# Decoder step on one core: affine maps of the decay gate and PSUM copies of the attention put on ScalarE instead of VectorE

## The chip, the cores and the metric

The kernel runs on one core of one Trainium2 chip. A core has a matrix engine (TensorE, PE in the profile, with its weight loads as PEld), VectorE (DVE), ScalarE (ACT), GpSimd (POOL) and SyncE (SP), which here issues all DMAs. The engines run their own queues in order and meet at semaphores. Matrix products are written to banks of PSUM; everything else lives in SBUF or in DRAM. The metric is the device time of one execution in microseconds, as the median of several runs.

## What is computed

One layer of a decoder for 512 prompt tokens and 8 x 8 new tokens (64 more columns), model width 1024, all in float32. Cut to what the change touches:

```python
u = x * (1 + sc1) + sh1
proj = u @ w_in            # qa, ka, va, qh, fh, ih, ogh, gate_a, gate_b
# attention: three groups (window, dilation) of four heads each
for gi, (win, dil) in enumerate(ATTN_GROUPS):
    # prompt: banded causal attention per residue; also returns the log-sum-exp
    # new tokens: keys of the cache and of the new tokens
    o_g, lse_g = attention(q_g, k_g, v_g)
attn = sum over groups of softmax(lses) * outs
# gated linear recurrence, eight heads
hq = silu(qh)
f = lb + (1.0 - lb) * sigmoid(fh)
hk = 1.0 - f
S_t = diag(f_t) S_{t-1} + hk_t v_t^T;  o_t = S_t^T hq_t
# merge by sigmoid gates, layer norm, squared-ReLU MLP, layer norm
```

Besides the layer's result, the keys and values of the prompt's last tokens and the caches moved on by the new tokens are outputs, so keys are needed with tokens along the partitions ("token-major") as well as the other way.

## The kernel before

Activations are kept with channels along the 128 partitions and the 576 tokens (`NT`) along the free axis, in two halves of 288 (`HF`). A float32 product is made of three products in a faster format: an operand is split into a rounded part and its rest (`whi`, `wlo` for weights, `uh`, `ul` for activations). `whi` is a copy on ACT, `wlo` a subtraction on DVE; both must be done before PE can begin a block of weights. `split` does this, and `ahead` calls it up to two blocks before the block runs.

The first part of the program runs over `flat`, a list of blocks of 128 columns of `w_in`, then of the two branch matrices. `run_block` does one: two halves of 24 matmuls into a PSUM bank tagged `lin` (two banks), each followed by `evac`, which takes the result out of PSUM, and after both an `after` that hands over side work. Of the attention, each group has `q_block`, `v_tokens` and `k_block`; of the recurrence, each head has `hq_block` (query), `hf_block` (decay), `hi_tokens` (values, for four heads at a time) and `ho_block` (output gate).

Side work is written as generators, one per item, in lanes of `Side`: `prompt_att(g, h)` (prompt attention of one head), `new_tokens(g)` (new tokens against new tokens), `sample_near` and `sample_far(g)` (new tokens against the cache), `hgrn(h)` (the recurrence of one head), `prompt_merge` and others. After every eight or so matmuls of the main blocks `pump` runs a step of a lane if the lane has credit and is due. `sample_far` makes its scores on POOL, a 128x512 product (`qb`) for each query row, and sums them on DVE (`sc`).

The order of all engines' queues is decided when the program is built. Every instruction goes through a proxy (`Engine`, line 111) that books it on its engine's own clock, with a fixed cost and a cost per element; a lane is due when the booked end of what it waits for has passed on PE's booked clock. The costs are

```python
    V, A = Engine(nc.vector, "DVE", 65.0, 1.05), Engine(nc.scalar, "ACT", 90.0, 0.84)
    G, PE, SP = Engine(nc.gpsimd, "POOL", 60.0, 2.28), Engine(nc.tensor, "PE", 0.0, 0.0), Engine(nc.sync, "SP", 0.0, 0.0)
```

Stores are put in a list and issued by SP when their source's booked end has passed, or when over 12 wait. Loads of weights go through three buffers (`wraw`), each freed when its `whi` and `wlo` have been made.

In the names of the profile the tiles that matter are:

- `ktm`: token-major keys of one head of the prompt, copied out of a `tr` bank after four transposes (one for group 0), and stored (lines 613 to 623). Nothing else reads them.
- `Op`: the output of one head's prompt attention, copied out of an `att` bank (lines 673 to 679). It is stored to DRAM scratch for groups 1 and 2 and kept for group 0; `prompt_merge` weighs and adds the three.
- `qp`: the new tokens' queries of a group, reordered from batch-major to token-major in two copies (lines 801 to 804). PE reads them in the next step of `new_tokens`.
- `kns`: the new tokens' keys, token-major, copied out of a `tr` bank and stored (lines 805 to 811).
- `hf`, `hk`: the decay f and 1 - f of one head. ACT takes the tanh of half the argument out of PSUM, half by half; after the second half one instruction makes f of it, with a scale and a bias per channel (`lbt`), and a second one makes 1 - f (lines 1167 to 1171).

`prompt_att` runs 12 times, `new_tokens` three times, `hf_block` eight times.

Of the kernel before, what the change touches and what calls it, by code (L numbers as in the profile page):

```python
# [14 lines left out]
AF = mybir.ActivationFunctionType  # L15
OP = mybir.AluOpType
# [10 lines left out]
NH = 4  # L27
# [218 lines left out]
def decoder_step(ctx, tc, I, O):  # L246
# [13 lines left out]
    V, A = Engine(nc.vector, "DVE", 65.0, 1.05), Engine(nc.scalar, "ACT", 90.0, 0.84)  # L260
# [7 lines left out]
    def page(shape, name, dtype=F32):  # L268
        return pages.tile(shape, dtype, name=name, tag="page")

    def bank(shape, tag, bufs=2):
        return psum.tile(shape, F32, name=tag, tag=tag, bufs=bufs)
# [220 lines left out]
    lbt = consts.tile([128, 4, 8], F32, name="lbt")  # L493
# [76 lines left out]
    qs, ks = {}, {}  # L570
# [35 lines left out]
    def prompt_att(g, h):  # L606
        q, k, vtm = qt.pop((g, h)), kt_.pop((g, h)), vt[g]
        if h == NH - 1:
            vt.pop(g)
        sl = float(SLOPES[g, h])  # L610
        Mx = bias_of[C_M0][:, cmask[g]:cmask[g] + (256 if g == 0 else 128)]

        kp = bank([128, 4, 128], "tr")
        for c in range(4):
            if g or c == 3:
                PE.transpose(kp[:, c], k[:, c * 128:(c + 1) * 128], ident)
        ktm = page([128, 4, 128], "ktm")
        if g:
            V.tensor_copy(ktm, kp)
        else:  # L620
            V.tensor_copy(ktm[:, 3], kp[:, 3])
        yield (436 if g else 109), 0
        keys_out(g, ktm, h)
        nm = stat_p[:, g, :, 0, h]
        ls = stat_p[:, g, :, 1, h]
        if g == 0:
            P = [page([128, 2, 256], "P") for _ in range(2)]
            sp = bank([128, 2, 256], "att")
            PE.matmul(sp[:, 0, 128:256], q[:, 0:128], k[:, 0:128], start=True, stop=True)
            PE.matmul(sp[:, 1], q[:, 128:256], k[:, 0:256], start=True, stop=True)  # L630
            V.scalar_tensor_tensor(P[0][:, 0, 128:], Mx[:, 128:], sl, sp[:, 0, 128:], op0=OP.mult, op1=OP.add)
            V.scalar_tensor_tensor(P[0][:, 1], Mx, sl, sp[:, 1], op0=OP.mult, op1=OP.add)
            yield 640, 0
            sp = bank([128, 2, 256], "att")
            PE.matmul(sp[:, 0], q[:, 256:384], k[:, 128:384], start=True, stop=True)
            PE.matmul(sp[:, 1], q[:, 384:512], k[:, 256:512], start=True, stop=True)
            V.scalar_tensor_tensor(P[1], Mx[:, None, :].to_broadcast([128, 2, 256]), sl, sp, op0=OP.mult, op1=OP.add)
            V.tensor_reduce(nm[:, 0:1], P[0][:, 0, 128:], axis=AX.X, op=OP.max)
            V.tensor_reduce(nm[:, 1:2], P[0][:, 1], axis=AX.X, op=OP.max)
            V.tensor_reduce(nm[:, 2:4], P[1], axis=AX.X, op=OP.max)  # L640
            tls = [(0, P[0][:, 0, 128:]), (1, P[0][:, 1]), (2, P[1][:, 0]), (3, P[1][:, 1])]
        else:
            P = page([128, 4, 128], "P")
            sp = bank([128, 4, 128], "att")
            for c in range(4):
                r = slice(c * 128, (c + 1) * 128)
                PE.matmul(sp[:, c], q[:, r], k[:, r], start=True, stop=True)
            V.scalar_tensor_tensor(P, Mx[:, None, :].to_broadcast([128, 4, 128]), sl, sp, op0=OP.mult, op1=OP.add)
            V.tensor_reduce(nm, P, axis=AX.X, op=OP.max)
            tls = [(c, P[:, c]) for c in range(4)]  # L650
        V.tensor_scalar(nm, nm, -1.0, None, op0=OP.mult)
        for c, p in tls:
            A.activation(p, p, AF.Exp, bias=nm[:, c:c + 1], accum_out=ls[:, c:c + 1])
        yield 870, None

        if g == 0:
            pairs = [(0, 0, P[0][:, 0, 128:])]
            for c in range(1, 4):
                pp = P[c // 2][:, c % 2]
                pairs += [(c, c - 1, pp[:, :128]), (c, c, pp[:, 128:])]  # L660
        else:
            pairs = [(c, c, P[:, c]) for c in range(4)]
        PT = []
        for a in range(0, len(pairs), 4):
            n = min(4, len(pairs) - a)
            tp = bank([128, 4, 128], "tr")
            for b in range(n):
                PE.transpose(tp[:, b], pairs[a + b][2], ident)
            t = page([128, 4, 128], "PT")
            A.activation(t[:, :n], tp[:, :n], AF.Copy)  # L670
            PT += [t[:, b] for b in range(n)]
            yield 109 * n, (t,)
        op = bank([128, 4, 128], "att")
        for n, (c, kc, _) in enumerate(pairs):
            first = n == 0 or pairs[n - 1][0] != c
            last = n == len(pairs) - 1 or pairs[n + 1][0] != c
            PE.matmul(op[:, c], PT[n], vtm[kc][:, h], start=first, stop=last)
        ot = page([128, 4, 128], "Op")
        V.tensor_copy(ot, op)
        yield 218 * len(pairs), 0  # L680
        if g == 0:
            O0[h] = ot
        else:
            store(osc[g - 1][h].rearrange("(i r) d -> i r d", r=4), ot)
            if h == NH - 1:
                store(ssc[g - 1].rearrange("(i r) x -> i r x", r=4),
                            stat_p[:, g].rearrange("p r x h -> p r (x h)"))
        att_done[0] += 1
        if att_done[0] == 12:
            side.add("p", prompt_merge())  # L690
# [107 lines left out]
    def new_tokens(g):  # L798

        base = CACHE[g] - (8 if g < 2 else 0)  # L800
        qp = page([128, 2 * NH, 32], "qp")
        for e in range(2):
            V.tensor_copy(qp[:, e * NH:e * NH + NH].rearrange("p h (t b) -> p h b t", b=4),
                          qs[g][:, :, 32 * e:32 * e + 32].rearrange("p h (b t) -> p h b t", t=8))
        vn, kn = vsam.pop(g).rearrange("p h d -> p (h d)"), page([NS, NH * 128], "kns")
        tp = bank([64, NH, 128], "tr")
        for h in range(NH):
            PE.transpose(tp[:, h], ks[g][:, h], ident)
        V.tensor_copy(kn, tp.rearrange("p h d -> p (h d)"))
        for x, t in enumerate((kn, vn)):  # L810
            store(out_s[g][0, :, base:base + 8, x].rearrange("b t h d -> b t (h d)"), t)
        yield 436, 500
        for e in range(2):
            sp = bank([128, 64], "att")
            for h in range(NH):
                PE.matmul(sp[32 * h:32 * h + 32], qp[:, e * NH + h], ks[g][:, h],
                          start=True, stop=True, skip_group_check=True)
            sb = tiny([128, 64], "sbn")
            on = tiny([128, 130], "on")
            o = (2 * g + e) * 64  # L820
            V.tensor_add(sb, sp, bias_of[C_SBN][:, o:o + 64])
            softmax(sb, on[:, 128:129], on[:, 129:130])
            yield 250, None
            tp = bank([64, 128], "tr")
            PE.transpose(tp, sb, ident)
            pn = tiny([64, 128], "pn")
            A.activation(pn, tp, AF.Copy)
            yield 109, None
            op = bank([128, 128], "att")
            for h in range(NH):  # L830
                PE.matmul(op[32 * h:32 * h + 32], pn[:, 32 * h:32 * h + 32], vn[:, h * 128:(h + 1) * 128],
                          start=True, stop=True, skip_group_check=True)
            V.tensor_copy(on[:, 0:128], op)
            store(snew[g, e], on)
            Onew[g, e] = True
            yield 300, 0
        sam_done[0] += 1
        if sam_done[0] == 6:
            side.add("r", sample_merge())
# [322 lines left out]
    def hf_block(h):  # L1162
        t = page([128, NT], "hf")
        k = page([128, NT], "hk")
        hf_[h], hk[h] = t, k

        def evac(hf, ps):
            A.activation(hv(t, hf), ps, AF.Tanh, scale=0.5)
            if hf:
                V.tensor_scalar(t, t, lbt[:, 1, h:h + 1], lbt[:, 0, h:h + 1], op0=OP.mult, op1=OP.add)  # L1170
                V.tensor_scalar(k, t, -1.0, 1.0, op0=OP.mult, op1=OP.add)

        def after():
            if h % 4 > 1:
                side.add("p", hgrn(h))
        return dict(evac=evac, after=after)
# [449 lines left out]
    for i, (u, j) in enumerate(flat):  # L1626
# [18 lines left out]
        if n_run == 20:  # L1645
            for e in range(2):
                t = page([128, 4, 128], "lmf")
# [106 lines left out]
    for k in range(KT):  # L1754
        t = page([128, NT], "hT")
# [564 lines left out]
```

## Time and profile before

| | us |
|---|---|
| median of 3 runs | 1382.89 |
| lowest, highest | 1377.75, 1384.52 |
| profiled execution, its own time | 1378.02 |
| span of the profile (first to last instruction) | 1376.2 |

The profile's page has these rows on the order of the stages: the busy tenths of an engine in 40 slices of 34.4 us, the clock that PE was granted, and the DMA engines' load.

```profile
PE   6999999999999999999999999999899999999995
DVE  2457556558767886666655436547455744756858
ACT  2423333332332222332232442325455732744732
POOL 1232023027417573234343300002410000000005
PEclk9999999999999999999999999999999999999998
DMA  9789899789988977776454313331054433544512
```

The attention and the recurrence run beside the blocks of `w_in` in slices 3 to 22 (to about 760 us); then come the branch products, the output product and the MLP. The chain that ended last is named by engine as follows.

```profile
PE 76%; DVE 10%; DMA 5%; ACT 4%; issue 3%; POOL 1%; SPq 1%; DVEq 0%; POOLq 0%; ACTq 0%
```

A group in the profile reads: line, engine, operation, tile written <- tiles read, shapes (partitions x elements), count, then busy us and mean ns of one, then the engine's idle time just before and what ended it. All instructions carry line 175, that of the proxy, so groups are told apart by tile.

### The profile page before, as it was taken

What the parts mean: (1) busy time and instruction counts of PE and PEld (TensorE: products, weight loads), DVE (VectorE), ACT (ScalarE), POOL (GpSimd) and SP (SyncE); (2) the same over time, 40 slices, a digit from 0 to 9 for tenths busy, and PEclk for the clock granted to TensorE, in tenths of its full rate; (3) what the DMA queues carried; (4) which work ended last, traced back from release to release, by engine and by line L of the source; (5) the groups of instructions that cost most, each with busy time, mean ns of one, the idle gap of its engine ahead of it and who ended that gap; (6) DMA issues with size and microseconds to landing.
All of it is one profiled execution on the core that took longest, in us unless ns stands there. A gap on an engine that the chain in (4) does not pass through costs nothing.

```text
span 1376.2 us, 24394 instructions
## 1 busy us (share of the span) xinstructions
PE 1315.5 (96%) x9480; PEld 1209.6 (88%) x9480; DVE 840.3 (61%) x1674; ACT 519.9 (38%) x1161; POOL 324.7 (24%) x371
## 2 busy tenths in 40 slices
PE   6999999999999999999999999999899999999995
PEld 3889898899878887888989999998899999999994
DVE  2457556558767886666655436547455744756858
ACT  2423333332332222332232442325455732744732
POOL 1232023027417573234343300002410000000005
PEclk9999999999999999999999999999999999999998
DMA  9789899789988977776454313331054433544512
GB/s 306 246 309 323 270 299 355 242 273 324 281 290 286 317 252 242 231 252 200 138 167 141 100 62 123 130 123 62 0 177 153 169 138 117 206 161 154 215 61 69
DMA packets 186824, 274.11 MB, mean 199 GB/s; under 512 B 16012, under 2 KB 92628, under 8 KB 186196
## 3 DMA queue, kind: packets, MB, share of 16 engines
q1 hardware_dynamic: 186708, 272.54, 58.7%
q8 instruction: 75, 1.23, 0.4%
q14 instruction: 41, 0.34, 0.1%
HBM read 212.81 MB, written 76.46 MB: 210 GB/s over the span
## 4 chain that ended last, share of the span: by engine, by line
PE 76%; DVE 10%; DMA 5%; ACT 4%; issue 3%; POOL 1%; SPq 1%; DVEq 0%; POOLq 0%; ACTq 0%
PE lin L175 58%; PE att L175 9%; PE sx L175 6%; DVE wlo L175 4%; PE tr L175 3%; DMA wada<-in_w_ada_dram 2%; DVE res L175 1%; ACT whi L175 1%; ACT sn L175 1%; DMA qb<-qsc 1%; SPq L175 1%; ACT hdh L175 1%; DMA out_dram<-kv 1%; DVE Op L175 1%; DVE hf L175 1%
## 5 line engine op out<-in xcount | busy, mean ns | idle before, releaser
L175 DVE TENSOR_TENSOR wlo<-wraw,whi 128x512 fp32r<-128x512 f32 (+1 forms) x334 | 271.1, 849 | 122.9 <-ACT whi L175 120.0
L175 PE MATMUL lin<-uh,whi 128*128 128x288 f32 x992 | 298.7, 301 | 5.1 <-DVE hso L175 2.4
L175 PE MATMUL lin<-ul,whi 128*128 128x288 f32 x992 | 299.5, 302 | 1.2 <-DVE ul L175 1.2
L175 PE MATMUL lin<-uh,wlo 128*128 128x288 f32 x992 | 298.6, 301 | 1.9 <-DVE wlo L175 1.9
L175 ACT ACTIVATE whi<-wraw 128x512 fp32r<-128x512 f32 (+1 forms) x338 | 211.6, 676 | 118.6 <-PE lin L175 37.0
L175 PEld LDWEIGHTS lin<-ul,whi 128*128 128x128 f32 x992 | 188.0, 189 | 13.8 <-issue 11.0
L175 PEld LDWEIGHTS lin<-uh,whi 128*128 128x128 f32 x992 | 187.8, 189 | 11.3 <-issue 2.9
L175 PEld LDWEIGHTS lin<-uh,wlo 128*128 128x128 f32 x992 | 188.1, 190 | 6.6 <-issue 3.8
L175 POOL TENSOR_TENSOR qb<-qb,kv 128x512 f32<-128x512 f32 x96 | 128.5, 1355 | 203.5 <-PE att L175 65.1
L175 PE MATMUL lin<-hdl,whi 128*128 128x288 f32 (+1 forms) x448 | 133.5, 298 | 4.0 <-DVE hdl L175 4.0
L175 PE MATMUL lin<-hdh,whi 128*128 128x288 f32 (+1 forms) x448 | 134.1, 299 | 0.0
L175 PE MATMUL lin<-hdh,wlo 128*128 128x288 f32 (+1 forms) x448 | 133.2, 297 | 0.0
L175 PEld LDWEIGHTS lin<-hdl,whi 128*128 128x128 f32 x448 | 84.5, 189 | 4.7 <-DVE hdl L175 4.7
L175 POOL TENSOR_TENSOR wlo<-wraw,whi 128x512 fp32r<-128x512 f32 x4 | 6.4, 1603 | 331.5 <-ACT whi L175 331.5
L175 PEld LDWEIGHTS lin<-hdh,whi 128*128 128x128 f32 x448 | 84.5, 189 | 0.0
L175 PEld LDWEIGHTS lin<-hdh,wlo 128*128 128x128 f32 x448 | 84.4, 188 | 0.0
L175 PE MATMUL lin<-whi,uh 128*128 128x512 f32 x160 | 68.4, 428 | 1.3 <-ACT whi L175 1.1
L175 PE MATMUL lin<-wlo,uh 128*128 128x512 f32 x160 | 63.9, 400 | 1.9 <-DVE wlo L175 1.9
L175 DVE TENSOR_REDUCE sc<-qb 128x4 f32<-128x512 f32 x96 | 63.7, 678 | 2.6 <-POOL qb L175 2.4
L175 PE MATMUL lin<-whi,ul 128*128 128x512 f32 x160 | 63.1, 394 | 0.0
L175 PE MATMUL lin<-u2h,whi 128*128 128x288 f32 x176 | 53.0, 301 | 6.1 <-ACT whi L175 4.9
L175 POOL TENSOR_TENSOR hk<-hk,T 128x256 f32<-128x256 f32 (+1 forms) x48 | 40.2, 838 | 72.0 <-PE att L175 43.4
(421 smaller groups left out, 2884.5 us busy)
## 6 DMA issues: line engine op xcount, KB each, us to landing
wraw<-in_w_in_dram SPq DMA_DIRECT2D x42, 1024.0 KB
kv<-in_cache_kv_w_dram SPq DMA_DIRECT2D x144, 256.0 KB
qb<-qsc SPq DMA_DIRECT2D x96, 256.0 KB
wraw<-in_w_down_dram SPq DMA_DIRECT2D x18, 1024.0 KB
out_dram<-kv SPq DMA_DIRECT2D x64, 256.0 KB
wraw<-in_w_ada_dram SPq DMA_DIRECT2D x16, 1024.0 KB
wraw<-in_w_up_dram SPq DMA_DIRECT2D x16, 1024.0 KB
out_dram<-in_cache_kv_w_dram SPq DMA_DIRECT2D x32, 512.0 KB
```

The source lines that it names most:

```text
L175: return f(out, *args, **kw)
```

## The change

Seven instructions of the program text go from DVE (`V`) to ACT (`A`): copies become activations with the function Copy, and the two maps of the decay gate become activations with the function Identity and a scale and a bias. Counted by execution: 8 wide and 4 narrow `ktm`, 12 `Op`, 6 `qp`, 3 `kns`, 8 `hf` and 8 `hk`, 49 in all. Nothing else in the text is different; the planner books them on ACT's clock with ACT's costs.

```diff
@@ prompt_att @@
         ktm = page([128, 4, 128], "ktm")
         if g:
-            V.tensor_copy(ktm, kp)
+            A.activation(ktm, kp, AF.Copy)
         else:
-            V.tensor_copy(ktm[:, 3], kp[:, 3])
+            A.activation(ktm[:, 3], kp[:, 3], AF.Copy)
...
         ot = page([128, 4, 128], "Op")
-        V.tensor_copy(ot, op)
+        A.activation(ot, op, AF.Copy)
@@ new_tokens @@
         for e in range(2):
-            V.tensor_copy(qp[:, e * NH:e * NH + NH].rearrange("p h (t b) -> p h b t", b=4),
-                          qs[g][:, :, 32 * e:32 * e + 32].rearrange("p h (b t) -> p h b t", t=8))
+            A.activation(qp[:, e * NH:e * NH + NH].rearrange("p h (t b) -> p h b t", b=4),
+                         qs[g][:, :, 32 * e:32 * e + 32].rearrange("p h (b t) -> p h b t", t=8), AF.Copy)
...
-        V.tensor_copy(kn, tp.rearrange("p h d -> p (h d)"))
+        A.activation(kn, tp.rearrange("p h d -> p (h d)"), AF.Copy)
@@ hf_block @@
             A.activation(hv(t, hf), ps, AF.Tanh, scale=0.5)
             if hf:
-                V.tensor_scalar(t, t, lbt[:, 1, h:h + 1], lbt[:, 0, h:h + 1], op0=OP.mult, op1=OP.add)
-                V.tensor_scalar(k, t, -1.0, 1.0, op0=OP.mult, op1=OP.add)
+                A.activation(t, t, AF.Identity, scale=lbt[:, 1, h:h + 1], bias=lbt[:, 0, h:h + 1])
+                A.activation(k, t, AF.Identity, scale=-1.0, bias=1.0)
```

## Prediction

> **What bounds the kernel now.** I read the page first, then the busy time by stretches, then TensorE's own waits inside the stretch that the change touches.
>
> ```profile
> span 1376.2 us, 24394 instructions
> PE 1315.5 (96%) x9480; PEld 1209.6 (88%) x9480; DVE 840.3 (61%) x1674; ACT 519.9 (38%) x1161; POOL 324.7 (24%) x371
> ```
>
> TensorE (PE) is busy 96% of the span, so the change, which takes nothing from PE, can only win time in which PE stands idle or runs at a lower clock. Every moved instruction lies between 104 us (first `ktm`) and 642 us (last `hf`). The next view has, for a stretch, its length, then busy time and count of PE, PEld, DVE, ACT and POOL, then PE's granted clock, DMA share and GB/s.
>
> ```profile
> 100.00:760.00 660.00, 642.36 (x4687) 567.62 (x4686) 432.47 (x910) 203.07 (x551) 239.36 (x248) 0.99 0.78 258
> 300.00:525.00 225.00, 212.02 (x1516) 189.02 (x1514) 175.85 (x327) 68.28 (x175) 123.40 (x110) 0.97 0.89 295
> ```
>
> From 100 to 760 us PE idles 660.00 - 642.36 = 17.6 us, 13.0 of it (225.00 - 212.02) from 300 to 525 us, where VectorE (DVE) is busy 78% (175.85 of 225) and ScalarE (ACT) 30%. Who keeps PE waiting in 100 to 760 us (total, times, longest):
>
> ```profile
> PE att L175 <- DVE S L175: 3.2, 1, 3.2
> PE lin L175 <- DVE wlo L175: 2.5, 2, 1.9
> PE lin L175 <- DVE hso L175: 2.4, 1, 2.4
> PE att L175 <- DVE qp L175: 1.9, 1, 1.9
> PE tr L175 <- DVE Op L175: 1.4, 1, 1.4
> ```
>
> These five are 11.4 us, all on DVE: the engine that the change relieves is the one that is late. The stretches of 25 us around the longest waits add a second price:
>
> ```profile
> 325.00:350.00 25.00, 22.24 (x172) 19.92 (x171) 18.89 (x37) 9.10 (x27) 17.95 (x15) 0.93 0.93 329
> 400.00:425.00 25.00, 22.57 (x159) 19.93 (x158) 15.73 (x35) 6.37 (x14) 4.62 (x6) 0.93 0.70 231
> 450.00:475.00 25.00, 22.64 (x166) 19.96 (x165) 21.05 (x39) 6.89 (x21) 13.84 (x12) 0.93 0.91 302
> 500.00:525.00 25.00, 21.77 (x152) 18.06 (x150) 21.23 (x34) 7.11 (x21) 9.74 (x9) 0.93 0.72 241
> ```
>
> Each of these four holds one of the waits of 1.9 us or more, and in each the granted clock is 0.93: another 7% of 25 us = 1.75 us each, 7.0 in all. The ceiling of what this stretch can give is thus 17.6 + 7.0 = 24.6 us.
>
> **What leaves DVE and what it costs on ACT.** Groups of instructions by shape, on DVE (count | busy us, mean ns | idle just before):
>
> ```profile
> L175 DVE COPY Op<-att 128x512 f32<-128x512 f32 x12 | 8.2, 684 | 10.6 <-PE att L175 10.6
> L175 DVE COPY ktm<-tr 128x512 f32<-128x512 f32 x8 | 5.5, 683 | 4.3 <-PE tr L175 4.3
> L175 DVE COPY ktm<-tr 128x128 f32<-128x128 f32 x4 | 1.1, 286 | 2.0 <-PE tr L175 2.0
> L175 DVE COPY qp<-qs 128x128 f32<-128x128 f32 x6 | 2.5, 493 | 0.0
> L175 DVE COPY kns<-tr 64x512 f32<-64x512 f32 x3 | 2.0, 679 | 1.1 <-PE tr L175 1.1
> L175 DVE TENSOR_SCALAR hf<-hf,lbt 128x576 f32<-128x576 f32 x8 | 10.0, 1244 | 7.5 <-ACT hf L175 7.5
> L175 DVE TENSOR_SCALAR hk<-hf 128x576 f32<-128x576 f32 x8 | 5.1, 636 | 0.3
> ```
>
> DVE loses 49 instructions, 34.4 us busy, and 25.8 us in which they held its queue while waiting for PE or ACT. Its busy time in 100 to 760 us falls from 432.5 to 398. On ACT the nearest rows are:
>
> ```profile
> L175 ACT ACTIVATE uh<-xT,mod 128x512 fp32r<-128x512 f32 x8 | 6.5, 808 | 6.8 <-DVE mod L175 5.4 <-issue 1.4
> L175 ACT ACTIVATE hT<-hT,gbl 128x288 f32<-128x288 f32 x16 | 9.1, 615 | 3.3 <-DMA hT<-xsc 3.3
> L175 ACT ACTIVATE ath<-attn 128x576 fp32r<-128x576 f32 x4 | 2.7, 679 | 2.3 <-PE att L175 1.8 <-ACT whi L175 0.5
> L175 ACT ACTIVATE hktm<-tr 128x512 f32<-128x512 f32 x8 | 4.8, 598 | 7.8 <-PE tr L175 7.2 <-PE sx L175 0.5
> L175 ACT ACTIVATE ats<-tr 128x128 f32<-128x128 f32 x2 | 0.8, 402 | 1.6 <-PE tr L175 1.6
> ```
>
> The map of `hf` (a column each for scale and bias) goes by `uh` and `hT`: 808 + 64 x (808 - 615)/224 = 863 ns. The map of `hk`, with constants, lies between `ath` (679, no column) and 863; I take 770. The 23 wide PSUM copies (12 `Op`, 8 `ktm`, 3 `kns`) go by `hktm`, 598; the four narrow `ktm` at DVE's 286; `qp`, a permuting copy, by `ats`, 402. Sum: 8 x 0.863 + 8 x 0.770 + 23 x 0.598 + 4 x 0.286 + 6 x 0.402 = 6.9 + 6.2 + 13.8 + 1.1 + 2.4 = 30.4 us, so ACT goes from 203 to 233 us of 660, 35%. No DMA is added; the stores of `ktm`, `kns` and `Op` keep their sources and are issued by SP when these are due. PSUM's `att` and `tr` banks come free when ACT has copied.
>
> All of this lies beside PE's work. It reaches the end only where PE waits now, or where ACT becomes late. Three places are touched directly.
>
> **Place 1, 327 to 329 us**, ACT and DVE by time (start, length):
>
> ```profile
> 325.77 0.58 ACT L175 ACTIVATE PT<-tr 128x512 f32<-128x512 f32 x1
> 327.26 0.49 ACT L175 ACTIVATE PT<-tr 128x384 f32<-128x384 f32 x1 [0.91 <-PE tr L175]
> 325.38 2.39 DVE L175 TENSOR_TENSOR wlo<-wraw,whi 128x512 fp32r<-128x512 f32 x2 [0.91 <-ACT whi L175]
> 327.69 1.47 DVE L175 COPY qp<-qs 128x128 f32<-128x128 f32 x2
> ```
>
> PE waits 1.9 us for `qp`, which stands on DVE behind two `wlo`. On ACT the two copies (0.8 us) fit into the 0.91 us that it idles before 327.26. Saved: 1.9 and its clock, 1.75; I take off 0.3, since `kns` (0.6) may then stand in front of the second `PT`. Term: 3.3 us (0 to 3.65).
>
> **Place 2, 364 to 380 us**, DVE:
>
> ```profile
> 363.79 0.58 DVE L175 TENSOR_SCALAR hf<-hf,lbt 128x576 f32<-128x576 f32 x1 [2.29 <-ACT hf L175]
> 364.40 0.46 DVE L175 TENSOR_SCALAR hk<-hf 128x576 f32<-128x576 f32 x1
> ```
>
> Behind these two runs the merge of the prompt's three groups, up to the `Op` for which PE waits 1.4 us, and to a `wlo` (2.5 - 1.9 = 0.6 us). Without them it begins 1.04 us sooner. Term: 1.04 + 0.6 = 1.6 us (0 to 2.0; 0 if the merge then waits for its loads).
>
> **Place 3, 442 to 455 us**, POOL, DVE and ACT:
>
> ```profile
> 442.12 11.66 POOL L175 TENSOR_TENSOR qb<-qb,kv 128x512 f32<-128x512 f32 x9
> 445.28 5.91 DVE L175 TENSOR_SCALAR hf<-hf,lbt 128x576 f32<-128x576 f32 x1
> 452.58 2.35 DVE L175 TENSOR_TENSOR wlo<-wraw,whi 128x512 fp32r<-128x512 f32 x2
> 446.82 1.15 ACT L175 ACTIVATE whi<-wraw 128x512 fp32r<-128x512 f32 x2 [4.00 <-DMA wraw<-in_w_in_dram]
> ```
>
> `hf`, 0.58 us elsewhere, takes 5.91 beside nine back-to-back multiplies on POOL, and the `wlo` behind it comes late: PE waits 1.9 us and loses 1.75 of clock. With `hf` and `hk` on ACT, `wlo` can begin at 447.4, 5 us sooner. Term: 3.6 us (0 if `wlo` is held up by POOL in the same way).
>
> Off these goes 0.5 us for new waits on ACT. Behind an `Op` that waits for PE stand the score exponentials, `qT` and the next `whi`, and PE waits for those; but ACT idles 457 of these 660 us. **Sum: 3.3 + 1.6 + 3.6 - 0.5 = 8.0 us.** The profiled execution took 1378.02 us (its span and 1.8 around it), so it would take 1370.0. The median before, 1382.89, lies 4.87 above that execution; with the same distance the time is **1374.9 us**, 0.58% less.
>
> A rule weighed here: the Trainium skill, "TensorE: Matmul & The Clock Gate", section "Why this matters for your kernels", asks for no PE idle gaps over about 3 us, after which the clock halves. By it the waits of 1.9 us would cost no clock, and the sum would be 8.0 - 3.5 = 4.5 us, 1378.4. The four rows at 0.93 speak against the figure: three of the four waits are under 3 us.
>
> The size that I can't work out is the order. The program's order is made by a planner that books every instruction on its engine's clock (DVE 65 + 1.05 n ns, ACT 90 + 0.84 n), so from 104 us on, side work, stores and loads can be put elsewhere. That redraws all of the stalls: down to the ceiling's rest (another 16.6 us), up by some two more waits like `S` (3.2 + 1.75 each, 10 us). I take 0, as a less loaded DVE makes neither likelier.
>
> **Rivals.**
>
> ```profile
> 496.39 7.94 POOL L175 TENSOR_TENSOR qb<-qb,kv 128x512 f32<-128x512 f32 x6
> 498.63 6.24 DVE L175 TENSOR_TENSOR wlo<-wraw,whi 128x512 fp32r<-128x512 f32 x2
> 357.29 2.18 ACT L175 ACTIVATE whi<-wraw 128x512 fp32r<-128x512 f32 x4
> 658.06 3.39 PE lin L175 x24
> ```
>
> *The stalls move.* At 498.63 two `wlo` alone took 6.24 us beside six POOL multiplies, with nothing of the change there, and PE's wait for `S` follows. If `wlo` takes `hf`'s place at 445, place 3 gives nothing, and places 1 and 2 may come back elsewhere: about 3 us saved, 1380.
>
> *DVE's relief spreads.* A lighter queue also removes the waits for `hso` and `S`: 2.4 + 3.2 + 2 x 1.75 = 9.1 us more, 1365.8. For it: they are DVE's too. Against: none of the moved instructions stands just before either.
>
> *ACT becomes late (slower).* Place: the eight `hf` blocks. At 357.29 the `whi` of a coming block follow `hf`'s second tanh (0.41 us) at once; after the change 863 + 770 = 1.63 us stand between. Tanh, maps, two `whi` (1.15) and a `wlo` (0.68) then take 3.9 us, beside a block of two halves of 24 matmuls, at 3.39 us 6.8 us. It decides once ACT arrives over 2.9 us late: from there each head costs PE 1.63 us and, near 1.9, the clock's 1.75. At five of eight heads: 5 x 3.38 = 16.9, less the 8.0, is 8.9 us slower, 1391.8. Against: ACT is at 35% even then. The Trainium skill, "ScalarE: Activation LUTs", section "Rules for kernel authors", speaks for this rival: multiplies and adds belong on VectorE. For the maps the trace agrees (0.58 and 0.46 us on DVE against 0.863 and 0.770); for copies out of PSUM it doesn't (683 against 598 ns).
>
> **How the numbers follow.** Under 0.5% (6.9 us, about what a measurement of this kernel can tell from no change) counts as the same: 1376.0 to 1389.8. Forecast 0.42 (1369 to 1381; somewhat over half below 1376.0), stalls move 0.24 (1376 to 1385), relief spreads 0.13 (1361 to 1370), ACT late or a worse order 0.21 (1386 to 1398, most of it above 1389.8). Faster: 0.25 + 0.13 + 0.02 = 0.40; slower 0.17; same 0.43. The range, 1363 to 1392, leaves out the far ends of the last two.
>
> **What would show it.** Right: `hf`, `hk`, `Op`, `ktm`, `qp`, `kns` on ACT, about 30 us; DVE near 398 us in 100 to 760; PE's waits for `qp` and for the `wlo` at 454 gone, two of the four stretches at 0.93 back at 1.00; PE's idle time there near 13 us. Wrong: new PE waits released by ACT (`whi`, `PT`, `hktm`), waits for `S` or `wlo` at other places beside POOL's multiplies, or more than four stretches at 0.93.

## Result: slower by 0.8%, and where the time came from

The changed kernel takes 1392.8 us (median of six runs, 1388.16 to 1395.77), the kernel before in the same session 1381.52 (six runs, 1374.66 to 1386.35): a ratio of 1.0084 with a 95% interval of 1.0057 to 1.011. The forecast was 1374.9 us, a gain; the time lies just outside its range (1363 to 1392), on the other side of the kernel before. Executions of one kernel differ by some 12 us here, so a profile shows mechanisms, and sizes of a few microseconds are taken from the ratios.

The page of the changed kernel, span and engines:

```profile
span 1391.0 us, 24408 instructions
PE 1319.4 (95%) x9480; PEld 1213.7 (87%) x9480; DVE 818.3 (59%) x1625; ACT 547.4 (39%) x1210; POOL 325.3 (23%) x371
```

The work moved as it should: VectorE has 49 instructions and 22 us less, ScalarE 49 and 27.5 us more. The groups by shape on ScalarE, changed kernel:

```profile
L175 ACT ACTIVATE Op<-att 128x512 f32<-128x512 f32 x12 | 7.2, 599 | 14.1 <-PE att L175 12.0 <-POOL qb L175 1.7 <-ACT whi L175 0.4
L175 ACT ACTIVATE hf<-hf,lbt 128x576 f32<-128x576 f32 x8 | 7.0, 869 | 0.3
L175 ACT ACTIVATE hk<-hf 128x576 f32<-128x576 f32 x8 | 5.5, 686 | 0.3
```

With `ktm` (599 ns each, 4.8 us), `qp` (425, 1.9), `kns` (630, 1.9) and the narrow `ktm` (278, 1.1) that is 7.2 + 7.0 + 5.5 + 4.8 + 1.9 + 1.9 + 1.1 = 29.4 us, close to the 30.4 forecast. The time is lost elsewhere. Busy time by stretches, first of the changed kernel:

```profile
300.00:525.00 225.00, 212.28 (x1563) 188.72 (x1562) 170.17 (x316) 79.04 (x195) 127.93 (x119) 0.98 0.86 282
525.00:760.00 235.00, 219.31 (x1639) 187.29 (x1638) 134.62 (x321) 73.91 (x191) 73.27 (x95) 0.97 0.62 194
100.00:760.00 660.00, 630.76 (x4574) 556.43 (x4573) 404.60 (x844) 226.27 (x588) 233.88 (x240) 0.98 0.77 253
```

and the last stretches of the kernel before:

```profile
525.00:760.00 235.00, 231.62 (x1797) 198.43 (x1798) 141.40 (x350) 74.00 (x198) 83.68 (x113) 1.00 0.60 193
```

The stretch that the prediction spoke of, 300 to 525 us, is no worse: 212.28 us of TensorE (PE) where before had 212.02. From 525 to 760 us, where no term of the prediction lies, PE loses 231.62 - 219.31 = 12.3 us of busy time, and the granted clock falls from 1.00 to 0.97. The changed kernel's own waits of PE, 100 to 780 us (total, times, longest), name a tile that was not in the prediction's list:

```profile
PE sx L175 <- ACT moda L175: 11.7, 3, 7.2
PE lin L175 <- DVE hso L175: 4.6, 2, 3.0
PE tr L175 <- DVE Op L175: 3.9, 1, 3.9
```

The waits for `qp` and `wlo` are gone, as forecast. In their place stand 11.7 us for `moda`, a copy that the change does not touch: ScalarE brings the product of the conditioning weights out of PSUM, and PE transposes it. What held it up is read on three engines, by time. ScalarE of the changed kernel (start, length, instruction, in brackets the idle time before it and what ended it):

```profile
677.79 1.15 ACT L175 ACTIVATE whi<-wraw 128x512 fp32r<-128x512 f32 x2 [13.67 <-DMA wraw<-in_w_in_dram]
678.85 0.58 ACT L175 ACTIVATE moda<-sx 128x512 f32<-128x512 f32 x1
```

PE of the changed kernel:

```profile
666.96 1.92 PE L175 MATMUL sx<-wraw,cT 128*32 128x512 f32 x16
679.48 1.12 PE L175 MATMUL sx<-ident,moda 128*128 128x128 f32 x4 [7.21 <-ACT moda L175]
```

and the sync queue (SP) of the changed kernel:

```profile
653.72 1.05 SPq L175 DMA_DIRECT2D ssst<-sst  x2
...
660.61 2.84 SPq L175 DMA_DIRECT2D om<-ssst  x4
...
672.54 1.16 SPq L175 DMA_DIRECT2D wraw<-in_w_in_dram  x2
```

Read from the bottom up: the weight load `wraw` is issued at 672.54, behind 20 loads of `om` for the sample merge; the first `om<-ssst` is not issued before 660.61, as it reads what the `ssst` stores of 653.72 write. ScalarE's next instruction, `whi`, idles 13.67 us for that load. `moda` needs only matmuls that were done by 669, but it is queued behind `whi`, and PE's transposes are queued behind `moda`: 7.21 us. Some 80 us earlier a similar pattern costs PE another 4.3 us. There `whi` (at 592.71) idles 8.22 us for its load, ahead of which no `om` load stands, and a load of an activation table (1.28 us) and two short instructions also come before `moda`.

Both gaps of PE also cost clock (third figure from the end, changed kernel):

```profile
590.00:615.00 25.00, 20.58 (x144) 18.05 (x143) 15.88 (x35) 9.18 (x17) 9.39 (x12) 0.93 0.71 205
670.00:695.00 25.00, 17.79 (x137) 17.02 (x136) 10.24 (x36) 8.29 (x25) 0.69 (x1) 0.86 0.61 195
```

In the kernel before, the weight load of that place is ahead of the merge's loads (SP):

```profile
644.18 0.45 SPq L175 DMA_DIRECT2D wraw<-in_w_in_dram  x1
...
655.62 0.51 SPq L175 DMA_DIRECT2D om<-snew  x1
```

So the planner's order differs. Two theories could explain the loss: **the order** costs it, whoever does the copies; or **ScalarE**, with 29 us more, is late for `whi` and `moda`. The comparison of starts below counts PE's main-line matmuls (those with `whi` or `wlo`) and gives how much later than before the n-th of them starts, in us (e1 and e8 are two of the experiments below):

```
   n    before    changed    e1      e8
1400     310.4     -0.3     +1.0    -0.8
1600     352.4     -4.6     -3.6    -4.7
1900     417.0     +1.9     -0.8    +1.1
2300     500.5    +11.2     +0.5    +6.8
2500     571.0     +5.0     +0.3    +0.3
2600     595.4    +14.9     +0.3    +6.4
2900     672.7    +15.8     +0.3    -1.3
3600     806.8    +14.2     +0.3    -3.6
```

### The profile page after: what moved, and what is told of

It reads as the page before. It is cut to its first block, busy times and chain, and to the rows that moved or that the text cites. A ratio compares the mean times of both kernels' runs of the same rounds, so it can differ in the third digit from the quotient of the medians.

```text
span 1391.0 us, 24408 instructions
## 1 busy us (share of the span) xinstructions
PE 1319.4 (95%) x9480; PEld 1213.7 (87%) x9480; DVE 818.3 (59%) x1625; ACT 547.4 (39%) x1210; POOL 325.3 (23%) x371
## 4 chain that ended last, share of the span: by engine, by line
PE 71%; DVE 8%; DMA 8%; ACT 5%; issue 4%; SPq 2%; POOL 2%; DVEq 0%; POOLq 0%; ACTq 0%
PE lin L175 53%; PE att L175 8%; PE sx L175 6%; PE tr L175 4%; DVE wlo L175 2%; SPq L175 2%; DMA wraw<-in_w_in_dram 2%; DMA qb<-qsc 2%; DMA kv<-in_cache_kv_w_dram 1%; ACT whi L175 1%; POOL qb L175 1%; ACT sn L175 1%; DVE res L175 1%; DVE Op L175 1%; DMA sgl<-ssc 1%
## 5 line engine op out<-in xcount | busy, mean ns | idle before, releaser
L175 POOL TENSOR_TENSOR qb<-qb,kv 128x512 f32<-128x512 f32 x96 | 132.0, 1391 | 209.7 <-DMA kv<-in_cache_kv_w_dram 98.8
```

The costliest lines, as they stand in the source:

```text
L175: return f(out, *args, **kw)
```

## Experiments

For e1 to e4, e10 and e12 the moved operations go through a helper that names two engines: the one that does the operation, and the one on whose clock the planner books it. A kernel can then have the work of one version in the order of the other.

```diff
+    def moved(on, book, out, src, scale=None, bias=None):
+        aps = [x for x in (src, scale, bias) if isinstance(x, bass.AP)]
+        end = book.enter([out], aps, book.fixed + book.rate * out.free_size(), 60.0)
+        Engine.top = max(Engine.top, end)
+        if on is A:
...
-        V.tensor_copy(ktm, kp)
+        moved(A, V, ktm, kp)
```

**e1: all 49 operations on ScalarE, in the old order** (`moved(A, V, ...)` throughout; the instruction sequences of PE and SP are those of before).

> The 49 instructions run on ScalarE as in the changed kernel, but the planner books them on VectorE with VectorE's costs, so that every queue but those two keeps the order of before. Theory 'order' (the time was lost where the planner, with the new bookings, put DMAs and side work elsewhere): ratio to before 0.990 to 1.000; the three terms of the prediction, 8 us, can now show themselves, 1373 of 1381 us. Theory 'ScalarE late' (the work itself delays ScalarE's queue, and the waits for moda, 11.7 us, are its own): ratio 1.005 to 1.012, with the same waits for moda.

Measured: 1377.65 us, 0.9978 (0.9963 to 0.9992). **e2: the reverse, all 49 on VectorE in the new order** (`moved(V, A, ...)`; PE and SP as in the changed kernel).

> The reverse: the 49 instructions stay on VectorE, but the planner books them on ScalarE, so that the other queues have the order of the changed kernel. Theory 'order': ratio to before 1.006 to 1.020, with PE's waits for moda near 11 us again. Theory 'ScalarE late': 0.996 to 1.003, no waits for moda.

Measured: 1400.36 us, 1.0133 (1.0108 to 1.0159). PE's first wait there, with nothing moved to ScalarE:

```profile
PE sx L175 <- ACT moda L175: 9.8, 3, 6.2
```

The two make a table of two by two: the work alone gains 0.22% (3 us), the order alone costs 1.33% (18 us), both together 0.84%. The theory of a late ScalarE falls: the `moda` waits are there without the moved work, and the moved work without the order is not slower.

**e3 and e4: half of the change each, with the order that the planner gives it.** e3 moves the 16 maps alone, e4 the 33 copies alone.

> Only the 16 maps of the decay gate go to ScalarE and are booked there; the 33 copies stay on VectorE. Theory 'order': an order of its own from 350 us on, so a time that does not follow from the share of the work moved, anywhere from 0.990 to 1.015. Theory 'ScalarE late': the maps are 12.4 of 30.3 us moved, so 0.4 of the loss, ratio 1.003.

> Only the 33 copies (ktm, Op, qp, kns) go to ScalarE and are booked there; the maps stay on VectorE. Theory 'order': again an order of its own, from 104 us on, 0.990 to 1.015. Theory 'ScalarE late': 0.6 of the loss, ratio 1.005, and the two losses add up to that of the whole.

Measured: e3 1381.45 us, 0.9999 (0.998 to 1.0018), without a `moda` wait; e4 1394.14 us, 1.0097 (1.0072 to 1.0122). The order that costs comes with the copies.

**Which copy?** The traces show it. How many of PE's 9480 matmuls and of SP's 787 DMA issues stand elsewhere than in the kernel before, by a line-by-line comparison of the two sequences (e5 and e6 are described below):

```
                             matmuls   DMA issues
changed kernel                   875           74
e3, the maps                      14            1
e4, the copies                   858           76
e5, Op alone                     858           76
e6, everything but Op             39            2
```

The twelve `Op` copies redraw the order by themselves. By the code, an operation pushes the clock that it is booked on to the end of what it waits for, here the value matmuls of a whole head, and with it all that is booked on that clock later; with `Op` on ScalarE's clock, other side work counts as due (this is read from the code, not measured). e5 moves only `Op`; e6 is the change without it; e7 does all that the change does, but books `Op` on VectorE's clock.

```diff
e5 (from the kernel before)
-        V.tensor_copy(ot, op)
+        A.activation(ot, op, AF.Copy)
e6 (from the changed kernel)
-        A.activation(ot, op, AF.Copy)
+        V.tensor_copy(ot, op)
e7 (from the changed kernel)
-        A.activation(ot, op, AF.Copy)
+        Engine.top = max(Engine.top, V.enter([ot], [op], V.fixed + V.rate * ot.free_size(), 60.0))
+        nc.scalar.activation(ot, op, AF.Copy)
```

> Only the prompt attention's output copy Op (12 copies) goes to ScalarE, the other 37 operations stay on VectorE; the planner redraws its order by itself, and that order is nearer to the changed kernel's than to the old one. Theory 'one booking redraws the order': this single edit brings nearly the whole loss, 1388 to 1402 us against 1381, with a PE wait of over 3 us for ScalarE's moda copy somewhere after 525 us. Rival 'the loss needs all the moved work or comes from the later orders': 1378 to 1385 us and no moda wait over 2 us.

> The change without its Op copies, which stay on VectorE: 37 operations go to ScalarE, and the planner's order comes out near to that of before. Theory 'one booking redraws the order': no moda wait over 1 us, and the time is that of the moved work in the old order, 1374 to 1380 us (0.995 to 0.999). Rival 'every redraw costs': 1383 to 1393 us.

> All 49 operations run on ScalarE as in the change, but the planner books the 12 Op copies, and only these, on VectorE's clock; TensorE's order is the same as with the Op copies left on VectorE. Theory 'one booking redraws the order': 1374 to 1380 us, no moda wait over 1 us; the difference to the kernel with Op on VectorE is under 3 us, and says what the Op copies alone are worth. Rival 'ScalarE is late once Op is on it': 1384 to 1395 us with waits of PE for ktm or P that ScalarE ends.

Measured: e5 1395.58 us, 1.0107 (1.0077 to 1.0138), with two `moda` waits, of 7.8 us in all and 4.7 the longest, and a wait for `Op` of 5.1 us (1.4 in before). Twelve copies of 0.6 us lose as much as the whole change. e6: 1377.96 us, 0.998 (0.9961 to 0.9998). e7: 1379.77 us, 0.9996 (0.9977 to 1.0015); its interval overlaps that of e6, which has the same PE sequence. Neither has a `moda` wait over 0.3 us. As in e1, the work is harmless on either engine; where the planner books `Op` decides.

**e8: the changed kernel, in its own order, with the merge's loads behind the weights.** `om` loads are booked where they were, but put on the queue only after the next weight load (or ahead of the first use of `om`).

```diff
+    def load_late(dst, src):
+        SP.enter([dst], [src], 600.0, 2000.0, dst.free_size() * dst.shape[0] * 4)
+        late.append((dst, src))
...
         u["slots"].append((k0, kk, t))
         live[0] += 1
+        if not load_q or live[0] + len(leaving) >= NRAW:
+            issue_late()
...
-                    SP.dma_start(t[p0:p0 + n, col:col + src.shape[-1]], src)
+                    load_late(t[p0:p0 + n, col:col + src.shape[-1]], src)
```

> The changed kernel with its planned order, but the 20 loads of om of each sample merge are put on the sync queue behind the next weight load instead of ahead of it. Theory 'weights behind the merge's loads on the one queue': the PE wait for moda near 679 us falls from 7.2 us to under 2, its half-clock spell of 6.8 us goes or halves, and the time falls from 1392.8 to 1382 to 1388 us. Rival 'the weight buffers come free late, or the transfers themselves are slow': the wait stays over 5 us and the time at 1391 to 1395 us. The moda wait near 596 us, ahead of which no om load stands, stays at about 4 us under both.

Measured: 1381.16 us, 1.0007 (0.9984 to 1.0031), against 1.0084 for the changed kernel: 0.77%, some 10.6 us, won back by two changed positions on one queue: in the traces the other engines' sequences are those of the changed kernel, and on SP two weight loads stand ahead of 20 `om` loads each instead of behind them. The time is a little below the 1382 to 1388 us expected. SP and ScalarE of e8 at that place, and PE's waits:

```profile
648.09 0.38 SPq L175 DMA_DIRECT2D wraw<-in_w_in_dram  x1
648.57 0.53 SPq L314 DMA_DIRECT2D om<-snew  x1
```

```profile
655.59 1.15 ACT L175 ACTIVATE whi<-wraw 128x512 fp32r<-128x512 f32 x2
660.52 0.60 ACT L175 ACTIVATE moda<-sx 128x512 f32<-128x512 f32 x1 [3.79 <-PE sx L175]
```

```profile
PE tr L175 <- DVE Op L175: 3.9, 1, 3.9
...
PE sx L175 <- ACT moda L175: 2.1, 1, 2.1
```

`whi` no longer waits, `moda` now waits for PE instead of PE for it, and the 7.2 us are gone, and with them the lost clock: from 655 to 680 us it is 1.00. The `moda` wait near 596 us, expected to stay at 4, shrank to 2.1 in this execution; why was not tried. What still separates e8 (1.0007) from the same work in the old order (0.9978) was not taken apart: the waits for `Op` and `moda` above and one of 3.4 us for `S` are its candidates.

**Why the work gains only 3 us.** The sum was 8.0. e9 moves only the `qp` copies (place 1), e10 only the maps, in the old order (place 3), e12 both together.

```diff
e9 (from the kernel before; PE's order is unchanged, on SP three stores stand elsewhere)
-            V.tensor_copy(qp[:, e * NH:e * NH + NH].rearrange("p h (t b) -> p h b t", b=4),
+            A.activation(qp[:, e * NH:e * NH + NH].rearrange("p h (t b) -> p h b t", b=4),
e10
-                V.tensor_scalar(k, t, -1.0, 1.0, op0=OP.mult, op1=OP.add)
+                moved(A, V, k, t, -1.0, 1.0)
...
```

> Only the 6 copies of the new tokens' queries (qp) go to ScalarE; the planner's order stays that of before. The PE wait of 1.9 us for qp at 329 us and its half-clock spell go. Theory 'the lead is given back': TensorE is 3 to 4 us ahead of before until about 370 us and loses it by 405 us, at the merge's Op and at hso, whose ends are set by other work; the time is within 1 us of before (0.999 to 1.001). Rival 'the place is worth what was forecast' (1.9 + 1.75 - 0.3 = 3.3 us): 0.997 to 0.998.

> Only the 16 affine maps run on ScalarE, booked as VectorE's so that TensorE's order stays that of before. The forecast's place 3 (1.9 + 1.75 us at 455) is in these alone: by the forecast 0.997 to 0.998. Theory 'the wait is replaced': the wlo wait at 455 us goes, a wait of some 2.9 us for ScalarE's junk comes at 461 to 463 us in its place, and the time is within 1 us of before (0.999 to 1.001).

Measured: e9 1378.64 us, 0.9978 (0.9961 to 0.9995); e10 1379.3 us, 0.9981 (0.9963 to 1.0). By the medians that is 3.0 and 2.6 us, nearer to the forecast terms (3.3 and 3.6 us) than to the nothing that the theory of each expected; the intervals reach from next to nothing to over 5 us. But e1, with both, had no more than either.

> The qp copies and the 16 affine maps together run on ScalarE, booked as VectorE's, so TensorE's order is that of before; Op, ktm and kns stay on VectorE. Alone the copies gave 0.9978 and the maps 0.9981. Theory 'the two places add': 0.9955 to 0.9965 (1375 to 1376.5 us). Rival 'what one place gives is lost at the next wait, so any of them gives the same 3 us': 0.9975 to 0.9985, with waits of over 2.5 us for hso near 404 us and for S or Oh near 505 us that are longer than in before.

Measured: 1379.53 us, 0.998 (0.9961 to 0.9999), which is in the rival's range. The two medians added would give 0.9959, just outside this interval, but they have wide intervals of their own: the times alone do not settle that the terms don't add. The profiles show where a gain goes. PE's waits in e12, 100 to 780 us:

```profile
PE lin L175 <- DVE hso L175: 3.4, 1, 3.4
PE att L175 <- DVE S L175: 3.2, 1, 3.2
PE att L175 <- ACT junk L175: 2.9, 1, 2.9
```

The waits for `qp` and for the `wlo` of 454 us are gone, but `hso` has grown from 2.4 to 3.4 us, and `junk` is new; `S` is as long as in before, not longer as the rival had it. Starts of the main-line matmuls as in the table above, in us against before:

```
   n    before      e1      e9     e10     e12
1400     310.4    +1.0    +1.4    -0.6    +2.7
1600     352.4    -3.6    -3.5    -0.4    -0.6
1800     396.6    -1.9    -0.4    -0.6    +0.5
1900     417.0    -0.8    -1.0    -0.2    +1.5
2100     461.6    -3.2    -0.9    -3.9    -2.3
2200     482.4    +0.5    -0.9     0.0    +1.4
2500     571.0    +0.3    -3.3    -0.2    +1.3
```

Place 1 lies between n = 1400 and 1600, place 3 between 1900 and 2100: PE gains there what was forecast, and soon after it has lost it. Of the 3.6 us in e1, 1.7 go at the merge of the prompt's groups, between 367 and 397 us: PE waits 1.8 us for `Op` and 2.0 for `wlo` there, 1.4 and 0.7 in before. POOL and VectorE of e1:

```profile
373.88 2.04 POOL L175 TENSOR_TENSOR og<-og,mw 128x512 f32<-128x512 f32 x2 [5.63 <-DMA og<-osc]
374.95 2.31 DVE L175 TENSOR_TENSOR Op<-Op,og 128x512 f32<-128x512 f32 x2 [1.71 <-POOL og L175]
```

and POOL of the kernel before:

```profile
375.30 2.49 POOL L175 TENSOR_TENSOR og<-og,mw 128x512 f32<-128x512 f32 x2 [3.77 <-DMA og<-osc]
```

PE comes 3.6 us sooner, the merge's load lets POOL begin only 1.4 us sooner, and `wlo` stands behind the merge on VectorE. Another 0.9 us go at `hso`, which ends at 404.8 in before and 403.9 in e1. e9 loses its lead at the same merge (3.1 us for `Op`, and a spell of lower clock). Most of what it has at 571 us comes later, at `S`: PE waits 2.4 us there instead of 3.2, and the clock does not fall this time. So the profiles don't lead the medians' 3 us back to the places, and where these come from is not shown; the profiled execution of before (1378.02 us) is itself some 3 us below the medians of before.

The gain of place 3 goes at the next wait. VectorE of e10 from 448 us:

```profile
448.98 2.74 DVE L175 TENSOR_TENSOR wlo<-wraw,whi 128x512 fp32r<-128x512 f32 x2 [3.76 <-ACT whi L175]
...
457.42 2.85 DVE L175 TENSOR_TENSOR wlo<-wraw,whi 128x512 fp32r<-128x512 f32 x2
460.20 0.68 DVE L175 COPY Oh<-att 128x512 f32<-128x512 f32 x1
```

and POOL and PE of e10:

```profile
457.24 2.49 POOL L175 TENSOR_TENSOR S<-S,T 128x512 f32<-128x512 f32 x2 [3.11 <-PE tr L175]
```

```profile
462.57 0.65 PE L175 MATMUL att<-vm,ksm 96*128 96x512 f32 x1 [2.87 <-ACT junk L175]
```

VectorE of the kernel before at that place:

```profile
460.51 1.28 DVE L175 TENSOR_TENSOR wlo<-wraw,whi 128x512 fp32r<-128x512 f32 x2
461.71 0.69 DVE L175 COPY Oh<-att 128x512 f32<-128x512 f32 x1
```

The first `wlo` now starts 3.6 us sooner than in before (452.58) and PE does not wait for it. But the next thing that PE needs is a free bank of `att`, which `Oh` and `junk` have to read first. POOL's `S`, which in before began at 461.11, when the second pair of `wlo` was half done, now runs beside all of it; the pair takes 2.85 us instead of 1.28, `Oh` starts only 1.5 us sooner, and PE waits 2.87 us there.

**e11: shortening the queue ahead of `hso`.** From e6, the four subtractions that make `hvp` go to POOL, booked as before.

```diff
-                V.tensor_sub(t[64:96], vs[own], t[own])
+                nc.gpsimd.tensor_sub(t[64:96], vs[own], t[own])
```

> The change without its Op copies (1377.96 us, 0.998), in the same order of TensorE, with the 4 subtractions that make hvp on POOL instead of VectorE. On VectorE they stand ahead of hso in the queue, two of 0.68 us with two waits of 0.6 to 0.7 us for ScalarE's copies. Theory 'hso is late because of the queue ahead of it on VectorE': the PE wait for hso at 404 us falls from 3.6 us to 1 to 2, and the time to 1374 to 1377 us (0.995 to 0.997). Rival 'the lead would be lost further on anyway', at S near 503 us: the hso wait shrinks, the S wait grows by as much, and the time stays at 0.998.

Measured: 1381.8 us, 1.0008 (0.999 to 1.0026); the wait for `hso` rose to 4.1 us. Neither expectation held. VectorE of e11:

```profile
399.85 2.14 DVE L175 TENSOR_TENSOR wlo<-wraw,whi 128x512 fp32r<-128x512 f32 x2 [3.29 <-ACT whi L175]
401.91 1.52 DVE L175 TENSOR_TENSOR Op<-Op,mw 128x512 f32<-128x512 f32 x1
```

and POOL of e11:

```profile
397.35 2.63 POOL L1194 TENSOR_TENSOR hvp<-hvs,hvp 32x512 fp32r<-32x512 f32 x2 [14.67 <-issue]
400.07 2.82 POOL L175 TENSOR_TENSOR og<-og,mw 128x512 f32<-128x512 f32 x2
```

VectorE gained nothing but idle time: `wlo` needs ScalarE's `whi`, which stands behind four copies into `hvp`. And POOL, given the subtractions, ran its merge multiplies 7.5 us later than in e6 (392.56 there), beside `wlo` and `Op`: these took 2.14 and 1.52 us, against 1.29 and 0.69 in e6.

## Why the prediction was wrong, step by step

- **The price on the engines: right.** 29.4 us on ScalarE against 30.4; VectorE 404.6 us in 100 to 760, forecast 398.
- **Places 1 and 3: right in mechanism and, at the place, about right in size.** PE gains 3.3 to 4.9 us at place 1 (e1, e9, e12; the term was 3.3) and 2.4 to 3.8 at place 3 (e1, e10, e12; 3.6). The medians of e9 and e10, 3.0 and 2.6 us, agree with the terms, but in the profiles the local gain does not reach the end, so that agreement is not evidence for them. **Place 2: nothing came of it.** In e1 the waits for `Op` and `wlo` there grew from 2.1 to 3.8 us, as the merge then waits for its loads: the case for which the prediction itself gave 0. In the changed kernel the wait for `Op` is 3.9 us.
- **The sum 3.3 + 1.6 + 3.6 - 0.5 = 8.0: wrong.** In the old order the whole change gives 3 us. The terms were added as if PE, once ahead, stays ahead; e1 and e12 show it spending the lead at the merge, at `hso` and at `junk`. The rival "the stalls move" (about 3 us saved) comes nearest to the work without the new order, though not by its condition: at 449 us the `wlo` in `hf`'s place took 2.74 us beside POOL, but PE did not wait for it. The waits behind it grew.
- **"I take 0, as a less loaded DVE makes neither likelier": the step that failed.** The order alone costs 1.33%, 18 us, beyond even the upper bound of 10 us set for it. That bound priced two more waits like `S`. It did not follow the queues past which the order would move something, SP's above all: a weight load behind 20 small loads, a copy behind a `whi` that waits for those weights, PE behind the copy. The profile of before had the parts: SP's list by time and ScalarE's waits for `wraw`.
- **"ACT late or a worse order", 1391.8: nearly the right time by the wrong mechanism, so by luck.** Its chance of 0.21 (1386 to 1398) named a worse order too, and that half came true, but without a mechanism or a price beyond two waits like `S`. The only wait at an `hf` head is 1.3 us (`PE lin <- ACT hf`, once). ScalarE is late for `moda`, not through the added work but through a wait for weights at the head of its queue; e2 has that without the added work.
- **Of the signs named beforehand**, `qp` and the `wlo` at 454 gone, and ScalarE's 30 us, came true; PE's idle time near 13 us didn't (660.00 - 630.76 = 29.2), and five stretches of 25 us at a lower clock, instead of two, were the sign of "wrong".

Of the kernels tried, e1, e6, e9, e10 and e12 come out at 0.998; the intervals of e1, e6, e9 and e12 lie below 1. These four beat both kernels, e9 with an edit of six copies.

## What to carry to other kernels

Where a planner orders the program by booked engine clocks, an edit that moves an operation to another engine is two edits; separate them by booking it on the old engine, and compare the sequences of all queues, the DMA queue's too, before you price anything. In an engine's in-order queue look for the instruction that waits for a transfer, and ask who stands behind it: the copy that PE waits for may be ready and merely queued. Savings at several waits need not add up: the lead that one gives is lost at the next wait whose end other work sets, a load or another engine's queue.

## What the runs showed of the hardware

**What a gap of PE does to its clock is not set by its length alone.** PE in e10, and the clock in 25 us around it (third from the end):

```profile
328.48 0.32 PE L175 MATMUL att<-ks,qp 128*32 128x64 f32 x8 [1.85 <-DVE qp L274]
```

```profile
325.00:350.00 25.00, 22.25 (x170) 19.91 (x168) 20.30 (x38) 8.66 (x27) 18.28 (x14) 0.93 0.95 323
```

and the same of e9 at `hso`:

```profile
404.90 0.40 PE L175 MATMUL lin<-uh,whi 128*128 128x288 f32 x1 [3.27 <-DVE hso L175]
```

```profile
400.00:425.00 25.00, 21.73 (x165) 19.10 (x164) 15.95 (x36) 7.17 (x17) 4.62 (x6) 1.00 0.74 246
```

1.85 us lowered the clock, 3.27 us did not. So "wait + 1.75 us" is a price that a gap may or may not cost, and part of the 12 us by which executions differ: of e11's twelve the quickest, 1374.91 us, had a mean clock of 0.992 and the slowest, 1386.1, of 0.982 (an estimate: 0.010 of some 1315 us of PE's work is 13 us). What else decides is not shown. The Trainium skill, "TensorE: Matmul & The Clock Gate", section "Why this matters for your kernels", puts the limit at gaps of about 3 us. Neither row goes by that: the gap of e10 lies below it and lowered the clock, that of e9 lies a little above it and did not.

**A VectorE operation can be held for most of a burst on POOL.** The map of `hf`, 0.58 us alone, took 7.15 us in e9, and 5.91 in before, beside nine multiplies in a row on POOL. VectorE and POOL of e9:

```profile
444.29 7.15 DVE L175 TENSOR_SCALAR hf<-hf,lbt 128x576 f32<-128x576 f32 x1
```

```profile
441.14 11.41 POOL L175 TENSOR_TENSOR qb<-qb,kv 128x512 f32<-128x512 f32 x9
```

It began in the middle of the burst and outlasted several of the nine, each some 1.3 us long (11.41 / 9). That POOL is what holds it is inferred from the overlap in these two executions; no run took the multiplies away.
